# Recurrence of an RWKV-7 / attention hybrid block: products without state gathered, VectorE order pinned, preparing bursts placed behind scan steps

## Chip, core and metric

The kernel runs on one core of one Trainium2 chip. The metric is the device time of one launch in microseconds. Before the change three runs took 1697.61, 1698.09 and 1704.32 us; the median is 1698.09.

The engines of the core work from queues of their own: TensorE (PE; its weight loads are shown as PEld), VectorE (DVE), ScalarE (ACT), GpSimd (POOL) and SyncE (SP), which here only issues transfers. Each works its queue in order and waits on semaphores.

## What is computed

One transformer block over 1024 tokens of width 1024, batch 1: a modulated RMS norm, a large input projection, eight heads of causal attention with a forget gate, eight heads of an RWKV-7 recurrence, gated merging, and a convolutional feed-forward net. All inputs are float32. The change touches the recurrence alone:

```python
def step(state, inp):
    r_t, w_t, k_t, v_t, a_t, b_t = inp
    sa = jnp.einsum('bhvk,bhk->bhv', state, a_t)
    state = state * w_t[:, :, None, :] + sa[..., None] * b_t[:, :, None, :] + v_t[..., None] * k_t[:, :, None, :]
    y_t = jnp.einsum('bhvk,bhk->bhv', state, r_t)
    return state, y_t
...
_, y = lax.scan(step, state0, (tm(r_h), tm(w_h), tm(k_h), tm(v_h), tm(a_vec), tm(b_vec)))
```

The state of a head is a 64 x 64 matrix.

## The kernel before

**Units and chunks.** The recurrence is computed by chunks of 64 tokens. A unit is a pair of heads (`p`, 0 to 3) and half of the sequence (`hf`), so there are eight units, numbered `k`, each of eight chunks (`NCU`). The two heads of a pair lie on partitions 0 to 63 and 64 to 127 (`HS`). Within a chunk all depends on matrices that can be made without the state; the state then passes from chunk to chunk in a short serial scan.

**Two chains.** A unit has two parts, written as Python generators that emit instructions and yield a wait in nanoseconds of a planned clock:

- `pre(k, p, hf)` prepares. It loads the decays (`cum`, L738) and makes their running sum by a scan instruction on DVE (L741); normalises the keys (product `ssq`, then a row of full-size DVE operations, L757 to L773); makes the in-chunk products (`p`, two bursts, L782 to L791); sends the diagonal blocks through DRAM (`sm` to `M32`, L796 to L801), inverts the triangular 32 x 32 blocks in 31 steps of two DVE operations (`t`, L809, and `E`, L811), and sends the inverses back through DRAM (`se` to `TT`, L822); transposes (`vt`, `at`, `tb`), and makes `q` and `bs`. Its waits are 1275, 3400, 10500, 2200, 2200, 2000 and 3400 ns.
- `main(k, p, hf)` uses them. It transposes the inverse's blocks on DVE (`X`, L866), waits for the time `ready` that `pre` had set (its own time plus 46000 for the first unit, 38500 for the others, L802), finishes the inverse (`xi`, `zi`), makes `uw` and `mz`, whose results DVE adds into `Zt` and `Mt` (L904, L905), and runs the scan over chunks. Then come the group norm's sums `mu` and `va`. Its waits are 2360, 2000, 2970, 2400, seven of 1150, 700, 3400, 2700 and 3400 ns.

**A step of the scan.** The next state is `(sp)*pcd`, where `sp` accumulates in PSUM a product without state, `E` by `UV`, and one with it, `Mt` by `S0`; DVE scales it (S, L929). The output `yp` is accumulated likewise from `UV` by `E` and `S0` by `Zt`. The function `fixed(c)` issues the four products without state of chunk c (two heads, `sp` and `yp`): chunk 0's behind `mz`, chunk c + 1's behind the wait of 1150 that follows step c. `sp` and `yp` are one PSUM bank each.

**Who decides the order.** PE's order is the order of emission, made by the planner `Weave`: `now` is a planned clock that `mm` and `transpose` advance by fixed costs (L67 to L75, L142). `run` serves the chain that is due, the main chain first; when none is due, `fill` emits products of large projections from a queue (`rkv`, `qk`, `v` and gate projections, 213 ns of the planned clock for one of 512 columns) until the next is due. In that clock a group of `fixed` costs 320, the state products of a step 213, `xi` and `zi` 427 each, `uw` and `mz` 1707 each. A preparing chain may run at most two units ahead (`passed`), and waits with filling until its three projections are there (`got`). The orders on DVE, ACT and POOL are not written out here: the framework chooses them, under the data's dependencies and those that are added by hand (`add_manual_dep` without a semaphore, which fixes an order on one engine).

**After the recurrence** come attention, which takes the gate projections that are left between its own steps, and then the merge and the feed-forward net.

Of the kernel before, what the change touches and what calls it, by code (L numbers as in the profile page):

```python
# [12 lines left out]
ALU = mybir.AluOpType  # L13
# [10 lines left out]
NCU = NH // CH  # L24
# [11 lines left out]
NOSYNC = mybir.DependencyInfo(mybir.DependencyClass.NoSync, mybir.DependencyReason.DATA)  # L36
# [11 lines left out]
class Weave:  # L48
# [27 lines left out]
    def add(self, load, run):  # L76
        self.queue.append((load, run))

    def prefetch(self):
        while (self.first or self.queue) and len(self.loaded) < 1:  # L80
            load, run = (self.first or self.queue).popleft()
            self.loaded.append((load(), run))
# [30 lines left out]

        self.live.append([self.now + wait, 0, chain])

    def run(self, chains):

        self.live = [[self.now, 1 + i, g] for i, g in enumerate(chains)]
        while self.live:
            due = min((c for c in self.live if c[0] <= self.now), key=lambda c: (c[1], c[0]), default=None)  # L120
            if due is None:
                self.fill(min(c[0] for c in self.live))
                continue
            wait = next(due[2], None)
            if wait is None:
                self.live.remove(due)
            else:
                due[0] = self.now + max(wait, 0.0)
# [3 lines left out]
def hybrid_block(ctx: ExitStack, tc: tile.TileContext, a, out):  # L132
    nc = tc.nc
    weave = Weave()
    ctx.enter_context(tc.manual_schedule(engines={mybir.EngineType.PE}))

    def mm(o, lhsT, rhs, start, stop, more=False):

        weave.mm_cost(o, lhsT, rhs)
        nc.tensor.matmul(o, lhsT, rhs, start=start, stop=stop, skip_group_check=more)  # L140
# [8 lines left out]
    tt, stt, ts = nc.vector.tensor_tensor, nc.vector.scalar_tensor_tensor, nc.vector.tensor_scalar  # L149
# [19 lines left out]
    def C(name):  # L169
        o, k = CST[name]  # L170
        return cst[:, o : o + k] if o < NC1 else cst2[:, o - NC1 : o - NC1 + k]
# [163 lines left out]
    with ExitStack() as es:  # L335
# [26 lines left out]
        def rkv_items(p, hf):  # L362
            ts_ = {x: rkp.tile([128, NH], F32, tag=f"{x}{hf}", name=f"{x}{p}{hf}") for x in "rkv"}
            rkv[p, hf], got[p, hf] = [ts_[x] for x in "rkv"], 0

            def steps(w, x, t):
                if hf == 0:
                    last_col[p, x] = shp.tile([128, 1], F32, tag=f"pv{x}", name=f"pv{p}{x}")
                yield from shifted(w, t, hf, ts_[x], last_col[p, x], f"rkv{t}")
                got[p, hf] += 1  # L370

            for x, t in (("k", 4 + p), ("r", p), ("v", 8 + p)):
                yield (lambda t=t: w_in(12 + t)), (lambda w, x=x, t=t: steps(w, x, t))
# [16 lines left out]
        HS = (slice(0, 64), slice(64, 128))  # L390
# [318 lines left out]
            return ap.rearrange("p (c x) -> p c x", x=x)  # L709

        BKS = (slice(0, 2), slice(1, 3))
        state, units, passed = {}, {}, set()

        blk_r = rw.tile([128, 128], F32R, name="blk_r")
        nc.scalar.copy(blk_r, C("blk"))
# [9 lines left out]
        def pre(k, p, hf):  # L725
# [5 lines left out]
            def tmp(nm, w=NH, bufs=1, dt=F32):  # L731
                return rw.tile([128, w], dt, tag=nm, name=f"{nm}{n}", bufs=bufs)

            def chunk_tile(nm, bufs, *dims):
                return rw.tile([128, *dims], F32, tag=nm, name=f"{nm}{n}", bufs=bufs)

            cum = tmp("cum")
            nc.sync.dma_start(cum, d_lora[0, p, :, cs])  # L738
            al = tmp("al")
            nc.sync.dma_start(al, d_lora[1, p, :, cs])  # L740
            nc.vector.tensor_tensor_scan(cum, C("reset"), cum, initial=0.0, op0=ALU.mult, op1=ALU.add)  # L741
            el = chunk_tile("el", 1, NCU, CH + 1)
            nc.gpsimd.memset(el[:, :, 0:1], 1.0)
            nc.scalar.activation(el[:, :, 1:], c3(cum), AF.Exp, scale=-DEC)
# [25 lines left out]
            pcd = chunk_tile("pcd", 3, NCU)  # L770
# [8 lines left out]
            E = chunk_tile("E", 2, NCU, 2, 3, CH)  # L779
            QA = chunk_tile("QA", 2, NCU, 2, CH)  # L780
            UV = chunk_tile("UV", 2, NCU, 2, CH)
            for c0 in range(0, NCU, 4):  # L782
                ps = [gen(f"p1_{n}{h}{c0}") for h in range(2)]
                for c in range(c0, c0 + 4):
                    for h in range(2):
                        mm(ps[h][:, (c - c0) * 128 : (c - c0) * 128 + 128], bk[HS[h], c, BKS[h], :], ar[HS[h], :, c, :],
                           start=True, stop=True)
# [11 lines left out]
            M32 = chunk_tile("M32", 1, 32, 32)  # L799
            for g in range(4):  # L800
                nc.sync.dma_start(M32[g * 32 : g * 32 + 32, :, :], sm.rearrange("h c b s t -> (h c b) s t"))  # L801
            ready = weave.now + (46000 if k == 0 else 38500)  # L802
            E32 = chunk_tile("E32", 1, 8, 32)
            nc.gpsimd.tensor_copy(E32, C("einit").rearrange("p (j t) -> p j t", t=32))
            t32 = tmp("t32", 256)
            for s in range(31):
                J, W = s // 4 + 1, 31 - s
                tv = t32[:, 0 : J * W].rearrange("p (j w) -> p j w", w=W)
                tt(tv, E32[:, 0:J, s : s + 1].to_broadcast([128, J, W]),  # L809
                   M32[:, s : s + 1, s + 1 : 32].to_broadcast([128, J, W]), op=ALU.mult)  # L810
                tt(E32[:, 0:J, s + 1 : 32], E32[:, 0:J, s + 1 : 32], tv, op=ALU.add)  # L811
            se = scr.tile([2, NCU, 2, 32, 32], F32, tag="se", name=f"se{n}")
            for g in range(4):
                nc.sync.dma_start(
# [2 lines left out]
            TT = chunk_tile("TT", 2, NCU, CH)  # L817
# [37 lines left out]
        def main(k, p, hf):  # L855
# [3 lines left out]
            pcd, ar, E, QA, TT, bon, UV = (o[k] for k in ("pcd", "ar", "E", "QA", "TT", "bon", "UV"))  # L859


            X = rw.tile([128, NCU, 32], F32, tag="X", name=f"X{n}", bufs=1)
            B0 = (slice(0, 32), slice(64, 96))
            B1 = (slice(32, 64), slice(96, 128))
            for h in range(2):
                nc.vector.transpose(X[B0[h], :, :], TT[B0[h], :, 0:32])  # L866
            yield max(0, o["ready"] - weave.now)
            xi = gen(f"xi{n}")
            for c in range(NCU):
# [25 lines left out]
            Zt = rw.tile([128, NCU, CH], F32, tag="Zt", name=f"Zt{n}", bufs=1)  # L895
            Mt = rw.tile([128, NCU, CH], F32, tag="Mt", name=f"Mt{n}", bufs=1)
# [11 lines left out]
            yp = py.tile([128, NCU, CH], F32, tag="yp", name=f"yp{n}")  # L908
            sp = py.tile([128, NCU, CH], F32, tag="sp", name=f"sp{n}")
            S0 = state.get(p)  # L910

            def fixed(c):

                alone = hf == 0 and c == 0
                for h in range(2):
                    mm(sp[HS[h], c, :], E[:, c, h, 2, :], UV[:, c, h, :], start=True, stop=alone)
                for h in range(2):
                    mm(yp[HS[h], c, :], UV[:, c, h, :], E[:, c, h, 1, :], start=True, stop=alone)

            fixed(0)  # L920
            yield 2400
            for c in range(NCU):
                if S0 is not None:
                    for h in range(2):
                        mm(sp[HS[h], c, :], Mt[HS[h], c, :], S0[HS[h], :], start=False, stop=True)
                S1 = None
                if not (hf == 1 and c == NCU - 1):
                    S1 = rw.tile([128, CH], F32, tag="state", name=f"S{n}{c}", bufs=3)
                    ts(S1, sp[:, c, :], pcd[:, c : c + 1], None, op0=ALU.mult)  # L929
                if S0 is not None:  # L930
                    for h in range(2):
                        mm(yp[HS[h], c, :], S0[HS[h], :], Zt[HS[h], c, :], start=False, stop=True)
                if c + 1 < NCU:
                    yield 1150
                    fixed(c + 1)
                S0 = state[p] = S1
            passed.add((k, 1))

# [53 lines left out]
        def pre_chain():  # L992
            for k, (p, hf) in enumerate(order):
                while got[p, hf] < 3:
                    weave.step()
                yield from pre(k, p, hf)
                if p < 3:
                    weave.first.extend(rkv_items(p + 1, hf))
                yield 0

        def main_chain():
            for k, (p, hf) in enumerate(order):
                while (p, hf) not in units:
                    yield 200
                yield from main(k, p, hf)
                yield 0

        weave.run([main_chain(), pre_chain()])
    rk_st.close()


# [307 lines left out]
    for x in range(2):  # L1319
        for n in range(8):  # L1320
            if x or n:
                k = 8 * x + n + 1
# [157 lines left out]
    due = []  # L1480
# [248 lines left out]
    units = [(k, j) for k in ORDER for j in range(NP)]  # L1729
# [265 lines left out]
```

## Time and profile before

| quantity | value |
|---|---|
| median of three runs | 1698.09 us (1697.61 to 1704.32) |
| the profiled execution: time, span | 1704.73 us, 1703.0 us |
| mean granted TensorE clock | 0.983 |
| instructions | 26042 |
| recurrence, 160 to 657 us: PE busy | 479.29 of 497 us |
| attention, 657 to 869 us: PE busy | 199.46 of 212 us |
| merge and feed-forward, 869 to 1703 us: PE busy | 826.24 of 834 us |

How rows are read. A row of the timeline has the start in us, the duration, engine, source line, operation, out<-in by the program's names, shapes, and the number of instructions merged; in square brackets is the idle time of the engine just before, and what ended it. A row of a table of waits has who waited for whom, the total in us, the number of waits and the longest. A row of a table of windows has the window, its length, busy time with instruction count of PE, PEld, DVE, ACT and POOL, then the granted clock of PE, the DMA engines' share, and GB/s. A float32 product appears as two matmul instructions. A matmul's duration holds its latency; products in a row overlap, so their pace is the distance of their starts. L140 is the one line that issues all products but the transposes, so products are told apart by their names.

### The profile page before, as it was taken

The page shows a single profiled execution, that of the slowest core. Times are in us where ns is not written, and L with a number is a line of the kernel's source. Part 1 is how long each engine was busy: PE and PEld are TensorE (multiplying, and loading weights), DVE is VectorE, ACT ScalarE, POOL GpSimd, SP SyncE. Part 2 cuts the span into 40 slices and gives each one's busy share as a digit, 9 for nine tenths or more (in the row PEclk, how much of TensorE's full clock was granted, in tenths as well). Part 3 has the DMA queues.
Part 4 walks back from the last instruction along what each step waited for, and adds up shares of the span by engine and source line. Part 5 has one row for each costly group of instructions (what it writes and reads, how often), then busy time and mean ns, then how long its engine had stood idle before and what let it go on. Part 6 is the DMA issues. An engine that isn't in the chain of part 4 may idle for free.

```text
span 1703.0 us, 26042 instructions
## 1 busy us (share of the span) xinstructions
PE 1638.0 (96%) x9772; PEld 1342.0 (79%) x9772; DVE 1220.8 (72%) x2390; ACT 808.6 (47%) x1482; POOL 143.4 (8%) x175
## 2 busy tenths in 40 slices
PE   5899999998999998999999999999999999999998
PEld 4767777786877776988878888888888888888886
DVE  5776787778676633888877634897777777787677
ACT  5453334333444554766642323654444444454455
POOL 0010101110111003123112000000000000000000
PEclk8899999999999999999999999999999999999999
DMA  8487743533342326433277611132333233484463
GB/s 328 139 314 205 192 125 97 136 106 106 91 115 75 91 81 151 141 110 107 76 265 268 246 62 63 50 105 94 123 107 103 93 117 101 163 284 153 125 215 112
DMA packets 120974, 239.85 MB, mean 141 GB/s; under 512 B 39888, under 2 KB 48336, under 8 KB 120848
## 3 DMA queue, kind: packets, MB, share of 16 engines
q1 hardware_dynamic: 112896, 220.94, 40.0%
q0 software_dynamic: 7952, 17.25, 3.8%
q8 instruction: 77, 1.26, 0.3%
q14 instruction: 49, 0.40, 0.1%
HBM read 172.59 MB, written 65.54 MB: 140 GB/s over the span
## 4 chain that ended last, share of the span: by engine, by line
PE 79%; DVE 9%; DMA 6%; ACT 2%; issue 2%; SPq 1%; DVEq 0%; ACTq 0%
PE X L140 13%; PE D L140 12%; PE Y L140 6%; PE wo L140 5%; PE br L140 5%; PE gt L140 5%; PE rk_ps L140 4%; PE qk L140 4%; PE ps_rkv L140 4%; PE W L140 3%; PE lg L140 2%; PE v L140 2%; PE ov L140 2%; PE sp L140 2%; PE tp L144 2%
## 5 line engine op out<-in xcount | busy, mean ns | idle before, releaser
L140 PE MATMUL D<-op,op 128*128 128x512 f32 x924 | 209.8, 390 | 0.0
L140 PEld LDWEIGHTS D<-op,op 128*128 128x128 f32 x924 | 173.5, 188 | 36.2 <-DVE op L1258 0.3
L140 PE MATMUL X<-T_m,S 128*128 128x512 f32 x440 | 107.3, 390 | 0.2
L140 PEld LDWEIGHTS X<-T_m,S 128*128 128x128 f32 x440 | 82.5, 188 | 18.2 <-ACT x L1534 0.6
L1257 ACT CAST op<-g 128x512 fp32r<-128x512 f32 x77 | 47.8, 621 | 74.1 <-PE D L140 48.0
L1258 DVE TENSOR_TENSOR op<-g,op 128x512 fp32r<-128x512 f32 x77 | 53.0, 689 | 41.7 <-ACT op L1257 41.7
L1494 DVE SCALAR_TENSOR_TENSOR c<-ab,vec,c 128x512 f32<-128x512 f32 x88 | 65.9, 750 | 19.5 <-ACT c L1497 17.9
L809 DVE TENSOR_TENSOR t<-E,M 128x60 f32<-128x60 f32 (+24 forms) x248 | 57.9, 233 | 30.2 <-DMA M<-sm 24.9
L1458 DVE TENSOR_TENSOR S<-ur,S 128x512 fp32r<-128x512 f32 x66 | 45.5, 691 | 35.6 <-ACT S L1454 35.5
L263 DVE TENSOR_TENSOR lo_in<-raw_in,hi_in 128x512 fp32r<-128x512 f32 x84 | 56.5, 707 | 16.1 <-PE gt L140 13.9
L1454 ACT CAST S<-ur 128x512 fp32r<-128x512 f32 x66 | 41.0, 622 | 55.6 <-DVE ur L1447 30.6
L1458 DVE TENSOR_TENSOR A<-ur,A 128x512 fp32r<-128x512 f32 x64 | 44.1, 688 | 30.9 <-ACT A L1454 30.7
L261 ACT CAST hi_in<-raw_in 128x1024 fp32r<-128x1024 f32 x42 | 44.0, 1049 | 44.3 <-PE ps_rkv L140 16.0
L140 PE MATMUL Y<-T_h,A 128*128 128x512 f32 x264 | 63.5, 390 | 0.0
L140 PE MATMUL Y<-T_h,S 128*128 128x512 f32 x264 | 63.3, 390 | 0.0
L140 PE MATMUL X<-B_b,A 128*128 128x512 f32 x252 | 60.8, 391 | 0.0
L140 PE MATMUL W<-B_f,A 128*128 128x512 f32 x252 | 60.6, 390 | 0.0
L1079 ACT ACTIVATE P<-lg,nm 128x896 f32<-128x896 f32 (+3 forms) x64 | 47.4, 743 | 22.8 <-DVE nm L1075 22.6
L811 DVE TENSOR_TENSOR E<-E,t 128x60 f32<-128x60 f32 (+24 forms) x248 | 53.8, 217 | 5.8
L140 PEld LDWEIGHTS Y<-T_h,A 128*128 128x128 f32 x264 | 49.6, 188 | 10.3
L140 PEld LDWEIGHTS Y<-T_h,S 128*128 128x128 f32 x264 | 49.6, 188 | 10.3
L1454 ACT CAST A<-ur 128x512 fp32r<-128x512 f32 x64 | 39.9, 623 | 34.2 <-PE X L140 31.5
(473 smaller groups left out, 4169.0 us busy)
## 6 DMA issues: line engine op xcount, KB each, us to landing
raw_in<-in_w_in SPq DMA_DIRECT2D x50, 512.0 KB, 3.7
wm<-in_w_mod SPq DMA_DIRECT2D x48, 512.0 KB, 7.0
ur<-in_w_up SPq DMA_DIRECT2D x44, 512.0 KB, 4.2
g<-d_g SPq DMA_DIRECT2D x35, 512.0 KB, 4.0
d_g<-gs SPq DMA_DIRECT2D x44, 256.0 KB, 2.0
d_g<-c SPq DMA_DIRECT2D x33, 256.0 KB, 4.4
d_st<-qh SPq DMA_DIRECT2D x64, 128.0 KB, 2.5
d_gate<-gs SPq DMA_DIRECT2D x32, 256.0 KB, 2.9
```

Of the source, the lines that this page charges most:

```text
L140: nc.tensor.matmul(o, lhsT, rhs, start=start, stop=stop, skip_group_check=more)
L144: nc.tensor.transpose(o, i, eye)
L261: nc.scalar.copy(hi, raw)
L263: nc.vector.tensor_tensor(lo[:, c : c + NH], raw[:, c : c + NH], f32(hi[:, c : c + NH]), op=ALU.subtract)
L809: tt(tv, E32[:, 0:J, s : s + 1].to_broadcast([128, J, W]), M32[:, s : s + 1, s + 1 : 32].to_broadcast([128, J, W]), op=ALU.mult)
L811: tt(E32[:, 0:J, s + 1 : 32], E32[:, 0:J, s + 1 : 32], tv, op=ALU.add)
L1079: nc.scalar.activation(e[:, 0:n], lg[:, 0:n], AF.Exp, bias=nm[:, 0:1], accum_out=nm[:, 1:2])
L1257: nc.scalar.copy(hi, src)
L1258: tt(lo, src, f32(hi), op=ALU.subtract)
L1454: nc.scalar.copy(hi, src)
L1458: tt(lo, src, f32(hi), op=ALU.subtract)
L1494: stt(c, ab[:, x + hf * NH : x + hf * NH + NH], V("conv_w", 22 * x + i), c, op0=ALU.mult, op1=ALU.add)
```

## The change

Six edits, all in the recurrence and the planner:

- The products without state of all eight chunks are issued in one go behind `mz`, ahead of the wait of 2400; between two steps only the wait of 1150 is left. As they now all come before the first product that accumulates on them, only chunk 0's opens its bank (`start=c == 0`).
- The two transposes `X` of unit k (from the second unit on) must follow, on DVE, the last state S of the unit before.
- The decay scan of unit k (from the second on) must follow, on DVE, step 11 of the inverse of the unit before.
- The first unit's `ready` is 48500 instead of 46000.
- `Weave.run` has an argument `beside`, 2600 for the recurrence: if the main chain is due within that time and no main step has been emitted since the last filling, a due preparing chain is held, the time up to the main step is filled, and the preparing burst comes right behind that step.
- `skip_group_check` on the scan's products concerns a check at build time and changes no instruction.

```diff
-    def run(self, chains):
+    def run(self, chains, beside=0.0):
         self.live = [[self.now, 1 + i, g] for i, g in enumerate(chains)]
+        led = False
         while self.live:
             due = min((c for c in self.live if c[0] <= self.now), key=lambda c: (c[1], c[0]), default=None)
-            if due is None:
-                self.fill(min(c[0] for c in self.live))
+            lead = min((c[0] for c in self.live if c[1] < 2), default=None)
+            if due is None or (due[1] > 1 and not led and lead is not None and lead < self.now + beside):
+                self.fill(min(c[0] for c in self.live) if due is None else lead)
+                led = False
                 continue
+            led = beside > 0 and (led or due[1] < 2)
             wait = next(due[2], None)
...
-            nc.vector.tensor_tensor_scan(cum, C("reset"), cum, initial=0.0, op0=ALU.mult, op1=ALU.add)
+            i = nc.vector.tensor_tensor_scan(cum, C("reset"), cum, initial=0.0, op0=ALU.mult, op1=ALU.add)
+            if k:
+                tc.add_manual_dep(i.ins, placed["inverse"].ins.name, NOSYNC)
...
-            ready = weave.now + (46000 if k == 0 else 38500)
+            ready = weave.now + (48500 if k == 0 else 38500)
...
-                tt(E32[:, 0:J, s + 1 : 32], E32[:, 0:J, s + 1 : 32], tv, op=ALU.add)
+                i = tt(E32[:, 0:J, s + 1 : 32], E32[:, 0:J, s + 1 : 32], tv, op=ALU.add)
+                if s == 11:
+                    placed["inverse"] = i
...
             for h in range(2):
-                nc.vector.transpose(X[B0[h], :, :], TT[B0[h], :, 0:32])
+                i = nc.vector.transpose(X[B0[h], :, :], TT[B0[h], :, 0:32])
+                if k:
+                    tc.add_manual_dep(i.ins, placed["state"].ins.name, NOSYNC)
...
-            def fixed(c):
+            for c in range(NCU):
                 alone = hf == 0 and c == 0
                 for h in range(2):
-                    mm(sp[HS[h], c, :], E[:, c, h, 2, :], UV[:, c, h, :], start=True, stop=alone)
+                    mm(sp[HS[h], c, :], E[:, c, h, 2, :], UV[:, c, h, :], start=c == 0, stop=alone, more=True)
                 for h in range(2):
-                    mm(yp[HS[h], c, :], UV[:, c, h, :], E[:, c, h, 1, :], start=True, stop=alone)
-            fixed(0)
+                    mm(yp[HS[h], c, :], UV[:, c, h, :], E[:, c, h, 1, :], start=c == 0, stop=alone, more=True)
             yield 2400
             for c in range(NCU):
...
-                    ts(S1, sp[:, c, :], pcd[:, c : c + 1], None, op0=ALU.mult)
+                    placed["state"] = ts(S1, sp[:, c, :], pcd[:, c : c + 1], None, op0=ALU.mult)
...
                 if c + 1 < NCU:
                     yield 1150
-                    fixed(c + 1)
...
-        weave.run([main_chain(), pre_chain()])
+        weave.run([main_chain(), pre_chain()], beside=2600.0)
```

More of the change, by code (lines that the diff above doesn't have):

```diff
@@ L711, in hybrid_block @@
         BKS = (slice(0, 2), slice(1, 3))
-        state, units, passed = {}, {}, set()
+        state, units, passed, placed = {}, {}, set(), {}
         blk_r = rw.tile([128, 128], F32R, name="blk_r")
@@ L924, in main @@
                     for h in range(2):
-                        mm(sp[HS[h], c, :], Mt[HS[h], c, :], S0[HS[h], :], start=False, stop=True)
+                        mm(sp[HS[h], c, :], Mt[HS[h], c, :], S0[HS[h], :], start=False, stop=True, more=True)
                 S1 = None
@@ L928, in main @@
                     S1 = rw.tile([128, CH], F32, tag="state", name=f"S{n}{c}", bufs=3)
-                    ts(S1, sp[:, c, :], pcd[:, c : c + 1], None, op0=ALU.mult)
+                    placed["state"] = ts(S1, sp[:, c, :], pcd[:, c : c + 1], None, op0=ALU.mult)
                 if S0 is not None:
                     for h in range(2):
-                        mm(yp[HS[h], c, :], S0[HS[h], :], Zt[HS[h], c, :], start=False, stop=True)
+                        mm(yp[HS[h], c, :], S0[HS[h], :], Zt[HS[h], c, :], start=False, stop=True, more=True)
                 if c + 1 < NCU:
                     yield 1150
-                    fixed(c + 1)
                 S0 = state[p] = S1
```

## Prediction

> **What bounds the kernel now.** I read the page first, then the recurrence (160 to 657 us) by windows, by TensorE's waits, and by the timelines of TensorE (PE) and VectorE (DVE) around the longest waits.
>
> ```profile
> span 1703.0 us, 26042 instructions
> PE 1638.0 (96%) x9772; PEld 1342.0 (79%) x9772; DVE 1220.8 (72%) x2390; ACT 808.6 (47%) x1482; POOL 143.4 (8%) x175
> ```
>
> PE sets the pace. In the recurrence it is kept full by projection products (`ps_rkv`, `qk`, `v`, `gt`) that the planner pours into every planned wait, and that work must be done anyway. So a shorter or longer plan only moves projections from one stage to another; time is won where PE really stands still, or where the same products take PE longer. The waits of PE from 157 to 657 us, with total, count and longest:
>
> ```profile
> PE sp L140 <- DVE S L929: 8.6, 5, 3.5
> PE xi L140 <- DVE X L866: 3.0, 2, 1.6
> PE p L140 <- DVE bk L769: 2.0, 1, 2.0
> PE ps_rkv L140 <- DVE k L358: 1.6, 1, 1.6
> PE at L144 <- DVE E L789: 1.0, 1, 1.0
> ```
>
> Every one of them is for DVE, whose queue is in a fixed order. Its own idle time in the same stretch says why it is late:
>
> ```profile
> DVE t L809 <- DMA M<-sm: 24.9, 7, 6.7
> DVE X L866 <- DMA TT<-se: 23.3, 12, 4.9
> DVE cum L741 <- DMA cum<-d_lora: 10.8, 5, 5.5
> ```
>
> The worst place, DVE and then PE:
>
> ```profile
> 421.72 0.43 DVE L866 STREAM_TRANSPOSE X<-TT 32x256 f32<-32x256 f32 x1 [3.80 <-DMA TT<-se]
> 423.68 0.28 DVE L929 TENSOR_SCALAR S<-sp,pcd 128x64 f32<-128x64 f32 x1
> 424.02 0.47 PE L140 MATMUL sp<-UV,E 128*64 128x64 f32 x4 [3.46 <-DVE S L929]
> ```
>
> The next unit's transpose X stands in DVE's queue ahead of this unit's state S and waits 3.80 us for a transfer; S is behind it, and PE stands for 3.46 us. The second such place costs 2.35 us:
>
> ```profile
> 532.86 0.34 PE L140 MATMUL sp<-UV,E 128*64 128x64 f32 x4 [2.35 <-DVE S L929]
> ```
>
> And an idle PE pays again:
>
> ```profile
> 420.00:424.00 4.00, 0.56 (x3) 0.13 (x1) 2.22 (x6) 1.22 (x2) 0.00 (x0) 1.00 0.17 25
> 424.00:428.00 4.00, 3.98 (x26) 2.96 (x28) 2.33 (x5) 0.71 (x2) 0.00 (x0) 0.57 0.17 60
> 529.00:533.00 4.00, 1.65 (x10) 1.04 (x12) 1.43 (x4) 1.24 (x2) 0.40 (x1) 1.00 0.42 98
> 533.00:537.00 4.00, 4.00 (x30) 2.78 (x28) 3.57 (x7) 1.25 (x2) 0.00 (x0) 0.57 0.17 66
> 230.00:232.50 2.50, 0.28 (x6) 0.20 (x7) 2.13 (x5) 0.00 (x0) 0.00 (x0) 1.00 0.60 139
> 232.50:237.00 4.50, 4.50 (x40) 3.63 (x41) 3.75 (x14) 1.96 (x5) 0.19 (x1) 0.62 0.48 152
> ```
>
> These windows come in pairs: a stretch with a hole in PE at clock 1.00, then one at 0.57 or 0.62. The lost clock is 4 x 0.43 = 1.7 us, 1.7 us and 4.5 x 0.38 = 1.7 us.
>
> On the clock, the Trainium skill ("TensorE: Matmul & The Clock Gate", section "HAM oscillation — how this bites in real kernels") says not to leave gaps of more than about 3.4 us. By it only the 3.46 us hole would have cost clock, and the sum below would be 3.4 us smaller, ending near 1687. The trace differs: the clock fell after 2.35 us too (window 533 to 537 at 0.57), so I go by the windows.
>
> **The change part by part.** Sums are made against the profiled execution, 1704.73 us (span 1703.0).
>
> *Transposes X behind the last state.* No instruction is added; the two transposes of the next unit must follow the last L929 of this one. Both big holes go: 3.46 + 2.35 = 5.8 us and 2 x 1.7 = 3.4 us of clock. What is late next is X itself. In unit 3:
>
> ```profile
> 320.63 1.16 PE L140 MATMUL p<-ar,bk 64*128 64x128 f32 x16
> 371.39 0.44 DVE L866 STREAM_TRANSPOSE X<-TT 32x256 f32<-32x256 f32 x1 [0.55 <-DMA TT<-se]
> 380.59 0.69 PE L140 MATMUL xi<-X,E 32*32 32x32 f32 x32
> ```
>
> X is ready 8.8 us ahead of its user, 51.2 us after the second `p` burst that begins its chain of transfers and DVE steps. That is the cover. **-9.2 us.**
>
> *First unit's due time 46000 to 48500.* PE waits 3.0 us at `xi` (table of waits) and loses 1.7 us of clock (232.5 to 237). A product of 512 columns is 213 ns in the planner, so 2500 more are 12 products; on the chip 8 of them take 1.81 us:
>
> ```profile
> 656.95 1.98 PE L140 MATMUL rk_ps<-u_hi,hi_in 128*128 128x512 f32 x8
> 658.76 1.98 PE L140 MATMUL rk_ps<-u_lo,hi_in 128*128 128x512 f32 x8
> ```
>
> So 12 x 0.226 = 2.7 us of wanted work takes the place of 2.7 of the 3.0 us. **-4.4 us** with the clock.
>
> *Decay scan behind the inverse's step 11.* The `ps_rkv` wait of 1.6 us comes from here:
>
> ```profile
> 393.11 1.23 DVE L741 TENSOR_TENSOR_SCAN cum<-cst,cum 128x512 f32<-128x512 f32 x1 [2.98 <-DMA cum<-d_lora]
> 395.70 0.74 DVE L358 SCALAR_TENSOR_TENSOR k<-ps_rkv,omu,sh_rkv 128x512 f32<-128x512 f32 x1
> 396.36 0.22 DVE L811 TENSOR_TENSOR E<-E,t 128x69 f32<-128x69 f32 x1
> ```
>
> DVE stood 2.98 us for the scan's input, and the eviction of k behind it was late. The inverse was then at step 8 (69 = 3 x 23 elements), so step 11 lies past the landing and the scan no longer waits. Its two readers, the exponentials on ScalarE (ACT), are wanted only some microseconds later. **-1.6 us** (0 if the wait moves).
>
> *All products without state in one go.* Nothing is added: each unit still issues eight groups of four `sp`/`yp` products, now behind `mz`. One step and a burst, before:
>
> ```profile
> 316.06 0.34 PE L140 MATMUL sp<-UV,E 128*64 128x64 f32 x4
> 316.23 0.29 PE L140 MATMUL yp<-E,UV 128*64 128x64 f32 x4
> 316.44 0.33 PE L140 MATMUL sp<-S,Mt 64*64 64x64 f32 x4
> 316.61 0.28 PE L140 MATMUL yp<-Zt,S 64*64 64x64 f32 x4
> 316.82 1.16 PE L140 MATMUL p<-ar,bk 64*128 64x128 f32 x16
> 328.26 1.15 PE L140 MATMUL q<-UV,E 64*64 64x64 f32 x32
> 329.34 0.50 PE L140 MATMUL va<-Zts,blk_r 128*128 128x512 f32 x1
> ```
>
> A fixed group takes 316.44 - 316.06 = 0.38 us (eight matmul instructions, two to a float32 product), eight of them 3.04. In one stream the bounds are 3.04 (nothing saved) and the rate of `q`, 1.08 us for 32, so 2.16 for 64. I take the rate of the `sp` half, 0.17 for 4, so 2.7, being the same products: 0.35 per unit, **-3 us** over eight units (0 to -7). The fixed group no longer waits for the S before it; the state product does, behind the same planned 1150. The planner's sum is unchanged: 8 x 320 + 2400 ahead and 7 x 1150 within, against 320 + 2400 and 7 x (1150 + 320). So Zt and Mt get 2.2 us more cover, and a step shrinks by 0.38 us, from about 2.35 to 1.97.
>
> *Preparing bursts beside steps.* A burst of the lower chain now waits for the next step of the main chain if that is due within 2600. With its own costs and waits the preparing chain of a unit is 31.0 in the planner's units (waits 25.0, products 6.0), the main chain 37.4. Eight pieces held by about 1.3 each make 41: it then takes longer than the main chain and slips by 3 to 4 a unit from unit 3 on, eating the 8.8 us of cover, until the due time of 38500 holds the main chain back and projections fill. What remains can be an X late by 0 to 2.5 us in some of units 4 to 7: **+2 us** (0 to +17). Where a burst lies directly behind other short products, one way in and out of the projections is saved, about 0.1 us a side (the first two projections behind a step took 0.57 us, rows below, not 2 x 0.226). That can be so for `tb`/`q` behind `xi`: **-1 us** (0 to -2).
>
> ```profile
> 265.19 0.73 PE L140 MATMUL ps_rkv<-u_hi,hi_in 128*128 128x512 f32 x2
> 265.76 1.09 PE L140 MATMUL ps_rkv<-u_lo,hi_in 128*128 128x512 f32 x4
> ```
>
> *What stays.* The stage's planned length hardly changes, so I take the same number of gate projections in it; one more or fewer (48 products of 0.226, 10.9 us) moves between stages without changing PE's sum. The other three state waits, 8.6 - 5.8 = 2.8 us, come from full-size DVE steps of the next unit between two states; I leave them as they are (0 to -2.8, or worse: rival B). The 2.0 at `p` and 1.0 at `at` stay.
>
> Sum: -5.8 - 3.4 - 4.4 - 1.6 - 3 + 2 - 1 = **-17 us**, 1687.5 on the profiled execution. That execution is 6.6 us above the median of the runs, 1698.09, and just above the slowest, 1704.32. If the 6.6 is made of the very waits for transfers that go, the runs win 17 - 6.6 = 10.6; if it lies elsewhere, 17. So 1681 to 1687.5; I take **1684**.
>
> **Rivals.**
>
> *A, the late preparing chain.* X misses its user in units 4 to 7 by about 2.5 us each, and each hole costs 1.7 us of clock: 4 x 4.2 = 17, so 1701. For it: 51.2 us from `p` to X against a due time of 38.5 in the planner's units; a whole unit of 37.4 lasts 50.6 us on the chip (from the row below to `xi` at 380.59), so 38.5 is about 52: hardly any margin. Against: a DVE that no longer stands for X runs the inverse faster.
>
> ```profile
> 330.00 0.69 PE L140 MATMUL xi<-X,E 32*32 32x32 f32 x32
> ```
>
> *B, the slower side: DVE sets the scan.* DVE in two scan windows:
>
> ```profile
> 302.70:316.80 14.10, 14.10 (x135) 10.04 (x132) 11.51 (x40) 3.44 (x5) 1.28 (x1) 1.00 0.48 119
> 467.20:481.70 14.50, 14.50 (x172) 12.05 (x171) 13.51 (x46) 4.35 (x7) 1.28 (x1) 1.00 0.36 109
> ```
>
> In the second DVE is busy 13.51 of 14.5 us, and the steps are to be a sixth shorter. If DVE holds the steps at 2.35 us, PE idles 0.38 in 56 steps, 21 us: 1705. It decides for slower from 0.40 us a step (22.6 us above 1684); with one more 0.7 us operation ahead of each S it is 39 us, 1723. Against: the burst gives DVE 2.2 us ahead of the scan, and in the first window DVE is busy 11.51 of 14.1 us.
>
> *C, the waits only move.* The transfers are no earlier; DVE waits for TT or M elsewhere, and other evictions are late. The X and scan terms (10.8) halve and the stream saves nothing: 1684 + 5.4 + 3 = 1692.
>
> **How the numbers follow.** Forecast 0.60, A 0.12, B 0.12, C 0.16. For this kernel 0.5% is 8.5 us: faster is below 1689.6, slower above 1706.6. The forecast's own range is 1676 to 1691, so 0.56 of its 0.60 is faster; C gives 0.04 more, and the rest of C, of the forecast and A make 0.27 within; B, nearly all slower, with a little of A makes 0.13. The low end, 1672, has the stream at -7, the state waits gone and no new `xi` wait (-4 - 2.8 - 2 from 1681, rounded); the high end, 1702, takes in A and C.
>
> **What would show it.** After the change no X should wait in DVE's queue ahead of an S, and no window of the recurrence should have a clock under 1.00. The stream behind `mz` should take about 2.7 us and a step about 1.97. `xi` waits in units 4 to 7 would show A; many short `sp` waits for S, B. If the two holes go and the time stands, the error is in what I count as PE's own pace.

## The result, and the profile after

| | before | after |
|---|---|---|
| median, same chips | 1700.68 us (1697.61 to 1704.32, 4 runs) | 1719.43 us (1718.50 to 1721.73, 4 runs) |
| profiled execution, span | 1703.0 us | 1716.7 us |

The ratio is 1.011, with a 95% interval of 1.0088 to 1.0131: slower by 18.8 us in the medians, 35 us above the forecast and 17 above the top of its range.

The same stages by windows, before and then after. The first window is the recurrence, up to the end of its last gate projection (a gate, for short); the second is attention, up to the first product of the merge. The columns are window, length, busy time and count of PE, PEld, DVE, ACT and POOL, clock, DMA share and GB/s.

```profile
160.00:657.10 497.10, 479.39 (x4319) 382.18 (x4318) 336.43 (x963) 212.25 (x371) 57.82 (x79) 0.99 0.40 112
657.10:868.90 211.80, 199.28 (x1201) 173.84 (x1199) 164.27 (x323) 140.34 (x318) 49.64 (x61) 0.97 0.41 114
868.90:1703.00 834.10, 826.32 (x3700) 684.01 (x3700) 610.23 (x942) 374.62 (x669) 22.72 (x16) 1.00 0.42 144
```

```profile
160.00:672.50 512.50, 491.44 (x4403) 395.23 (x4402) 345.22 (x967) 222.45 (x387) 57.91 (x79) 0.98 0.39 111
672.50:881.00 208.50, 184.78 (x1104) 161.70 (x1103) 159.42 (x320) 130.43 (x298) 41.51 (x51) 0.94 0.37 106
881.00:1716.70 835.70, 828.00 (x3700) 684.72 (x3700) 610.33 (x942) 374.54 (x669) 23.26 (x16) 0.99 0.42 143
```

The recurrence is 15.4 us longer, attention 3.3 us shorter, the rest 1.6 us longer: 13.7 us, the difference of the spans. That is 5 us less than the medians differ, because the profiled execution of before, 1704.73 us, was slower than its other runs and the one of after, 1718.50, the fastest of its four. And the stages no longer hold the same work: by the counts attention has lost 97 matmul instructions and the recurrence gained 84; most of the difference had run ahead of 160 us already:

```profile
0.00:160.00 160.00, 133.00 (x556) 101.94 (x557) 109.86 (x165) 81.39 (x126) 13.21 (x20) 0.91 0.73 252
```

```profile
0.00:160.00 160.00, 135.92 (x568) 104.52 (x569) 110.68 (x167) 82.72 (x128) 13.66 (x20) 0.93 0.74 256
```

The gates emitted in the recurrence, before and after (the row has busy time, mean in ns, and the idle time before):

```profile
L140 PE MATMUL gt<-u_hi,hi_in 128*128 128x512 f32 x144 | 40.7, 407 | 0.0
```

```profile
L144 PE MATMUL gt<-u_hi,hi_in 128*128 128x512 f32 x176 | 47.8, 400 | 0.4 <-DVE r L362 0.4
```

A gate has 16 products of this kind (and 32 of the other two), so it is nine gates before and eleven after, with seven and five left for attention. Two gates are 96 x 0.226 = 21.7 us of PE. The recurrence took 84 x 0.226 = 19.0 us more work in 15.4 us, so it has saved only 3.6 us of its own. Attention gave up 21.7 us of work and got 3.3 us shorter: PE's idle time in it rose from 12.5 to 23.7 us, and its busy time fell by 14.5 us instead of 21.7, at a lower clock (0.97, then 0.94). Some of its waits, before and then after (who for whom, total us, count, longest):

```profile
PE rk_ps L140 <- ACT gm L1180: 4.7, 2, 4.5
PE ov L140 <- DVE o L1148: 3.2, 2, 2.2
PE lg L140 <- ACT P L1079: 0.6, 2, 0.4
```

```profile
PE ov L144 <- DVE o L1154: 7.3, 4, 2.3
PE rk_ps L144 <- ACT gm L1186: 4.6, 2, 4.4
PE lg L144 <- ACT P L1085: 3.6, 3, 1.9
PE ov L144 <- DVE tl L1121: 2.6, 3, 2.0
```

PE waits there for results of the softmax on ACT and DVE; gates fill PE between attention's own products. The last gate product of attention began at 859.5 us before and at 818.6 after. Two windows of 25 us from that part of the stage, before and then after:

```profile
800.00:825.00 25.00, 25.00 (x162) 22.43 (x161) 21.05 (x44) 19.33 (x44) 8.99 (x12) 1.00 0.43 128
825.00:850.00 25.00, 23.61 (x145) 20.42 (x144) 18.89 (x42) 15.14 (x38) 0.90 (x1) 1.00 0.06 22
```

```profile
816.00:841.00 25.00, 18.83 (x121) 17.22 (x120) 20.57 (x43) 16.35 (x37) 6.01 (x7) 0.92 0.33 97
841.00:866.00 25.00, 18.86 (x100) 16.46 (x99) 15.77 (x36) 11.28 (x30) 0.00 (x0) 0.84 0.00 1
```

With gates PE is busy 48.6 of 50 us; without them 37.7, and the clock falls to 0.92 and 0.84.

Why two more gates? The projections that a preparing chain needs are put at the head of the queue when an earlier preparing chain ends, behind what is running and what is already loaded. Whenever a queued projection starts, the next one is taken from the queue and loaded. Unit 3's preparation ends with `bs`. Before, then after, on PE's timeline:

```profile
334.43 0.50 PE L140 MATMUL bs<-cum,blk_r 128*128 128x512 f32 x1
334.77 0.40 PE L140 MATMUL bs<-en,blk_r 128*128 128x512 f32 x1
...
340.02 0.28 PE L140 MATMUL v<-hi_v,u_hi 128*128 128x256 f32 x1
```

```profile
332.97 1.11 PE L144 MATMUL v<-hi_v,u_hi 128*128 128x256 f32 x8
...
339.89 0.50 PE L144 MATMUL bs<-cum,blk_r 128*128 128x512 f32 x1
340.23 0.39 PE L144 MATMUL bs<-en,blk_r 128*128 128x512 f32 x1
```

Before, `bs` came ahead of the start of the first `v` projection, so what was loaded at that start was unit 5's. After, `bs` came 7 us behind it: the second `v` was loaded already and went ahead of the projections of unit 5. These ran from 416 us, not 382. All later units were late, three gates and not one slipped in ahead of the last set of unit projections, and the recurrence could not end before that set was used. Rows from the first and the last of these sets, before and then after:

```profile
382.51 1.78 PE L140 MATMUL ps_rkv<-u_hi,hi_in 128*128 128x512 f32 x7
...
515.79 1.98 PE L140 MATMUL ps_rkv<-u_hi,lo_in 128*128 128x512 f32 x8
```

```profile
416.22 2.00 PE L144 MATMUL ps_rkv<-u_hi,hi_in 128*128 128x512 f32 x8
...
514.22 2.00 PE L144 MATMUL ps_rkv<-u_hi,hi_in 128*128 128x512 f32 x8
```

The last products of the last set began at 515.79 before; after, its first began at 514.22.

The edits on DVE's order did much of what was expected. From 157 to 680 us after the change, DVE's idle time for M and TT, and PE's three largest waits:

```profile
DVE t L815 <- DMA M<-sm: 26.5, 7, 6.0
DVE X L874 <- DMA TT<-se: 13.2, 7, 4.1
```

```profile
PE sp L144 <- DVE S L936: 7.1, 5, 3.0
PE mz L144 <- ACT UV L903: 4.3, 1, 4.3
PE p L144 <- DVE bk L775: 2.7, 2, 1.5
```

X's idle time fell from 23.3 to 13.2 us, the decay scan's from 10.8 to 0.2, and the wait at `xi` is gone. But waits for S are still 7.1 us, and a new one stands at `mz`. There the late preparing chain makes it: the inverse, with its wait for M, now falls between `uw` and `mz`. On DVE:

```profile
388.64 0.19 DVE L815 TENSOR_TENSOR t<-E,M 128x31 f32<-128x31 f32 x1 [5.30 <-DMA M<-sm]
388.87 0.19 DVE L817 TENSOR_TENSOR E<-E,t 128x31 f32<-128x31 f32 x1
389.10 0.19 DVE L815 TENSOR_TENSOR t<-E,M 128x30 f32<-128x30 f32 x1
389.20 0.42 DVE L901 COPY Wt<-uw 128x256 f32<-128x256 f32 x1
```

The second Wt, which `mz` needs, stands behind the inverse's first operations, and these wait 5.30 us for M. The copy UV on ACT, which the table names, came later still: in the trace it waits 5.54 us for that Wt.

### The profile page after: what moved, and what is told of

It is laid out like the page before. It is cut to its first block, busy times and chain, and to the rows that moved or that the text cites. A ratio compares the mean times of both kernels' runs of the same rounds, so it can differ in the third digit from the quotient of the medians.

```text
span 1716.7 us, 26060 instructions
## 1 busy us (share of the span) xinstructions
PE 1640.1 (96%) x9772; PEld 1346.2 (78%) x9772; DVE 1225.6 (71%) x2394; ACT 810.1 (47%) x1480; POOL 136.3 (8%) x165
## 4 chain that ended last, share of the span: by engine, by line
PE 60%; DVE 6%; ACT 2%; DMA 1%; issue 1%; SPq 0%; DVEq 0%; ACTq 0%
PE X L144 13%; PE D L144 12%; PE Y L144 6%; PE wo L144 5%; PE br L144 5%; PE gt L144 5%; PE W L144 3%; PE rk_ps L144 3%; PE lg L144 2%; PE ov L144 2%; PE tp L148 2%; DVE nm L1081 1%; DVE P L1091 1%; PE tr L144 1%; DVE tl L1121 1%
## 5 line engine op out<-in xcount | busy, mean ns | idle before, releaser
L1263 ACT CAST op<-g 128x512 fp32r<-128x512 f32 x77 | 47.8, 621 | 74.0 <-PE D L144 47.5
L267 DVE TENSOR_TENSOR lo_in<-raw_in,hi_in 128x512 fp32r<-128x512 f32 x88 | 60.6, 723 | 27.8 <-PE gt L144 12.2
L1081 DVE TENSOR_REDUCE nm<-lg 128x1 f32<-128x896 f32 (+3 forms) x64 | 46.8, 752 | 14.5 <-PE lg L144 13.7
```

The costliest lines, as they stand in the source:

```text
L267: nc.vector.tensor_tensor(lo[:, c : c + NH], raw[:, c : c + NH], f32(hi[:, c : c + NH]), op=ALU.subtract)
L1081: nc.vector.tensor_reduce(nm[:, 0:1], lg[:, 0:n], axis=AX.X, op=ALU.max, negate=True)
L1263: nc.scalar.copy(hi, src)
```

## The experiments

Two theories stood against each other. G: the loss is attention's, which has lost two gates to a changed order of projections. H: the loss is in the recurrence, in waits that the holding of preparing bursts makes. "Held" below means that the bursts wait for a main step, as in the change. The number of gates in the recurrence is known ahead for each kernel from its order of emission.

**Two gates early, in the kernel before.**

```diff
-    while len(weave.queue) > 12:
+    while len(weave.queue) > 4:
```

> The kernel before, with one number changed: two more gate projections (96 products) are emitted between the recurrence and attention, so attention is left with five of them, as in the kernel after, instead of seven. Nothing in the recurrence differs. Theory G (the loss of the change is attention's lost filler): the two gates cost 96 x 0.226 = 21.7 us ahead of attention and attention gets only about 3 us shorter, so 1700.7 + 18 = 1719 (1714 to 1723). Theory H (the loss sits in the recurrence, in waits that the held preparing bursts make): work that only moves costs nothing, 1700.7 within 4.

Measured 1724.15 us against 1699.01 (ratio 1.0153, 1.013 to 1.0176): +25 us. That is 7 us more than G's 18 and just above its range, and far from H's nothing: gates moved ahead of attention are not free. Attention's window, from the end of the last gate ahead of it:

```profile
683.30:886.10 202.80, 182.79 (x1105) 160.06 (x1104) 157.88 (x317) 130.34 (x298) 40.08 (x50) 0.95 0.30 91
```

Attention shrank by 9 us here (211.8 to 202.8) for the 21.7 us of work taken from it. The stretch ahead of it grew by 26.2 us (523.3 against 497.1), with a wait of PE of 3.9 us for an eviction on DVE among the moved gates. So the two profiled executions (1721.89 and 1704.73 us) differ by 17 us, close to G's 18, and the medians by 25; the profiled one of before is slower than most of its runs.

**The kernel after with 46000.**

```diff
-            ready = weave.now + (48500 if k == 0 else 38500)
+            ready = weave.now + (46000 if k == 0 else 38500)
```

> The kernel after with the first unit's due time put back to 46000; the bursts are still held. By the order of emission nine gates then lie in the recurrence again, not eleven. Theory G: 1719.4 - 18 for the gates + 4.4 for the first unit's xi wait that comes back = 1706 (1700 to 1710). Theory H: the holding is still there and the xi wait comes back, so 1719 to 1726.

Measured 1690.96 us (ratio 0.9954, 0.994 to 0.9969). The kernel is faster than before, with the holding in it. H as the whole cause falls: its range began 28 us higher. G's number was 15 us too high as well. It took 18 us for the gates where the run above shows 25, and the `xi` wait that came back was 1.3 us, not 3.0; that is not all of the 15.

**The kernel after without holding.**

```diff
-        weave.run([main_chain(), pre_chain()], beside=2600.0)
+        weave.run([main_chain(), pre_chain()])
```

> The kernel after without the holding of preparing bursts (beside 0); gathered products, both orders on VectorE and 48500 stay. Nine gates in the recurrence by the order of emission. Theory G: 1719.4 - 18 = 1701, less what the gathered products and the orders save without holes made by the holding, so 1690 to 1701. Theory H: the same direction; only a time above 1710 would speak against both.

Measured 1680.45 us (ratio 0.9889, 0.9873 to 0.9905), 10 us below G's low end. Timed once more:

> The kernel after without holding, timed again on the chip of the run beside it: 1680 within 3.

Measured 1679.37 us against 1700.73 (ratio 0.9886, 0.9862 to 0.9909). This beats both kernels. Its recurrence and attention, and its three largest waits from 157 to 655 us:

```profile
160.00:632.20 472.20, 464.23 (x4306) 372.58 (x4306) 336.65 (x960) 211.05 (x369) 58.55 (x79) 1.00 0.41 116
632.20:840.70 208.50, 196.59 (x1200) 171.66 (x1199) 164.42 (x323) 140.38 (x318) 49.16 (x61) 0.98 0.40 115
```

```profile
PE rk_ps L144 <- ACT gm L1186: 3.6, 2, 3.0
PE p L144 <- DVE bk L775: 2.7, 2, 1.5
PE sp L144 <- DVE S L936: 2.2, 3, 1.0
```

The stage is 24.9 us shorter than before with the same nine gates (some 3 us of it had run ahead of 160 us, 13 instructions by the counts), its clock is 1.00, and the waits for S are 2.2 us. Attention takes 208.5 us, the same length as after the change, with 96 products more in it.

Set beside the kernel after, this shows that G is not all. The recurrence after is 40.3 us longer (512.5 against 472.2). Two gates are 21.7 of these; the other 18.6 us were lost inside the recurrence, where PE idles 21.1 us instead of 8.0 and the clock is 0.98.

**Holding alone, in the kernel before** (only the planner's loop and `beside=2600.0`).

> The kernel before with nothing but the holding of preparing bursts (beside 2600). Nine gates in the recurrence by the order of emission. Theory G: no great change, 1700.7 within 6, since the number of gates is that of before. Theory H: the holding itself makes waits, 1708 to 1720.

Measured 1701.27 us (ratio 1.0011, 1.0002 to 1.0021): +2 us, as G has it. In the kernel before holding costs little where the order of projections stays.

**Either side of the change of order.** The kernel after with two due times 500 ns apart.

```diff
-            ready = weave.now + (48500 if k == 0 else 38500)
+            ready = weave.now + (47000 if k == 0 else 38500)
```

> The kernel after with the first unit's due time 47000 in place of 48500; all else as in after. By the order of emission the second set of projections for unit 5 then comes ahead of the second v projection again, and nine gates lie in the recurrence. Theory G (attention's lost filler): like the run with 46000, with a smaller xi wait, 1686 to 1692. Theory H (the loss comes smoothly from holding together with a late first unit): between 1691 (46000) and 1719 (48500) by the distance, 1000 of 2500 ns, so about 1702.

Measured 1689.93 us (ratio 0.9939, 0.9915 to 0.9964), inside G's range.

> The same with 47500, 500 ns more in the planner than its neighbour. By the order of emission eleven gates lie in the recurrence. Theory G: a jump of about 25 us (the price measured for two gates emitted early), 1711 to 1720. Theory H: 500 ns are worth at most 6 us, about 1708 or less.

Measured 1712.07 us (ratio 1.0068, 1.0048 to 1.0088), inside G's range again. Half a microsecond in the planner cost 22 us. In the profiled executions the recurrence grew from 482.5 to 500.6 us and attention shrank only from 209.4 to 205.5. The end of unit 3's preparation and the `v` projections, with 47000 and then with 47500:

```profile
336.93 0.50 PE L144 MATMUL bs<-cum,blk_r 128*128 128x512 f32 x1
337.26 0.39 PE L144 MATMUL bs<-en,blk_r 128*128 128x512 f32 x1
...
337.72 1.11 PE L144 MATMUL v<-hi_v,u_hi 128*128 128x256 f32 x8
```

```profile
329.47 0.40 PE L144 MATMUL v<-hi_v,u_hi 128*128 128x256 f32 x2
...
333.71 0.50 PE L144 MATMUL bs<-cum,blk_r 128*128 128x512 f32 x1
334.04 0.39 PE L144 MATMUL bs<-en,blk_r 128*128 128x512 f32 x1
```

With 47000 `bs` came just ahead of the first `v` product; with 47500 `v` had begun 4.2 us earlier. This is the step between nine gates and eleven, and a smooth cost of holding would not make it. The last 1000 ns, from 47500 to 48500, add 7 us more (1712.1 to 1719.4) at eleven gates in both.

**Gathering alone, in the kernel before** (`fixed` for all chunks behind `mz`, as in the change).

> The kernel before with only the products without state gathered behind mz. Nine gates. In the trace of after the eight groups took 1.9 us in a stream, against 0.38 each before: 3.05 - 1.9 = 1.15 us less a unit, so theory S (stream) expects -9 us, 1690 (1686 to 1694). Theory B (VectorE sets the scan, as in the prediction): the shorter steps come back as waits for S, 1699 or more.

Measured 1691.38 us against 1699.51 (ratio 0.9954, 0.9936 to 0.9973): -8 us, as S has it. DVE did not take over the scan: PE's waits for S were 7.4 us, against 8.6 before.

**The two orders alone, in the kernel before** (both `add_manual_dep`).

> The kernel before with only the two orders on VectorE (transposes X behind the last state, decay scan behind step 11). Nine gates. The prediction's terms: -9.2 for the two holes and their clock, -1.6 for the scan: 1688 (1685 to 1691). Theory C (the waits only move): half of it or less, 1694 to 1699.

Measured 1688.34 us (ratio 0.9937, 0.9916 to 0.9959): -11 us, the size that was expected. PE's waits for S and X in the recurrence:

```profile
PE sp L140 <- DVE S L935: 4.8, 5, 2.2
PE xi L140 <- DVE X L870: 1.3, 1, 1.3
```

The waits for S fell by 3.8 us (from 8.6), not by 5.8; the wait at `xi`, which stood in another term, fell by 1.7. So the total fits better than its parts, and that is partly luck.

**48500 alone, in the kernel before.**

> The kernel before with only the first unit's due time at 48500. Nine gates. The prediction's term was -4.4 (the xi wait of 3.0 us with 1.7 us of clock, less 0.3 that stays): 1695 (1693 to 1697). If the clock loss is not real or another wait takes its place: 1698 or more.

Measured 1701.30 us against 1700.73 (ratio 1.0003, 0.999 to 1.0016): nothing. The `xi` wait is gone and another, of 4.0 us, is there:

```profile
231.26 2.93 PE L140 MATMUL qk<-u_hi,hi_in 128*128 128x512 f32 x6 [4.04 <-DVE v L358]
```

PE now reaches a PSUM buffer that the eviction of v had not freed: that eviction stands on DVE just behind the late X, at 230.45 us, and ends as PE goes on. The extra filling only met DVE's lateness elsewhere.

**Gathering and orders without the other two** (the kernel after, `beside=0`, 46000).

> The kernel after without holding (beside 0) and with 46000: the gathered products and the two orders alone. Nine gates. If the parts add: 1699.5 - 8.1 - 11.2 = 1680, and with 48500 on top (the earlier run, 1680.5) nothing more was won. If 48500 was worth its 4.4 there: 1684 to 1686 here. With this run the four of holding and due time are complete.

Measured 1684.91 us (ratio 0.991, 0.9884 to 0.9936). With 48500 beside it on the same chip 1679.37: here the due time was worth 5.5 us. The four combinations of holding and due time, with gathering and orders in all:

| | 46000 | 48500 |
|---|---|---|
| not held | 1684.9 | 1679.4 |
| held | 1691.0 | 1719.4 |

Held, the due time costs 28 us; not held, it saves 5.5. The four were not all timed together; the kernels before beside them lay within 2 us of each other.

## Why the prediction was wrong

- **The step that failed** is in the part "What stays": the planned length hardly changes, so the same number of gate projections lies in the recurrence, and "one more or fewer ... moves between stages without changing PE's sum". The number was eleven, not nine. PE's sum did stay (busy 1638.0 us before, 1640.1 after), but the time is not PE's sum: attention cannot use the time that the gates leave, so it becomes idle time, and two gates cost 25 us in the kernel before. The profile of before had the hint: attention's PE is busy 199 of 212 us with 76 us of gates in it (7 x 48 x 0.226), so without them it must idle.
- **Preparing bursts beside steps**, +1 us in the sum, was mis-sized and mis-placed. That the preparing chain slips was right, and so was the reason: with 48500 unit 3's `bs` came at 339.89 us held and at 329.59 not held. But I priced the slip by X against its cover (rival A, 17 us), not by what else hangs on the chain's end, which is the place of the next projections in the queue, nor by the inverse that now falls into the main chain. The waits at `xi` that would have shown A did not come. In the runs holding costs 2 us alone, 6 with gathering and orders (1691.0 against 1684.9), and 40 with 48500 as well; in the profiles that is about 22 for the two gates and 19 inside the recurrence.
- **Transposes and decay scan** (-9.2 and -1.6, together -10.8): measured -11.2. The mechanism and the total were right, the split between the waits was not (above).
- **Gathering** (-3, bounds 0 to -7): measured -8.1. The mechanism was right; the stream takes about 2.0 us for 64 matmul instructions (after: first at 289.99, next projection at 292.00), 31 ns each, faster than the 34 of `q` which I took as the lower bound. A step did come out as forecast: 1.96 us from one state product to the next (after: 299.51 to 301.48), for 1.97.

```profile
289.99 0.34 PE L144 MATMUL sp<-UV,E 128*64 128x64 f32 x4
...
292.00 1.42 PE L144 MATMUL qk<-u_lo,hi_in 128*128 128x512 f32 x5
```

- **48500** (-4.4): 0 alone, -5.5 with gathering and orders beside it, and +28 where bursts are held, most of it at the step in the order of projections.
- **Rival B** (DVE sets the scan) fell with gathering alone. **Rival C** (waits only move) fell for the orders, but describes 48500 alone well.
- Where the order of projections stayed, the held kernels won 8 us (46000) and 10 us (47000), about half of the sum's 17, and the kernel without holding 21. So the size of the sum was not confirmed for the kernel that it was made for.

What is not shown: that in the kernel after, with 48500 and 2600 unchanged, restoring the order of projections alone would give two gates' worth of time back. No run did that; the pair 500 ns apart and the two gates moved in the kernel before stand for it. Which waits make up the 18.6 us inside the recurrence, beyond those at S and `mz`, is open too.

## What to carry to other kernels

Filler work is not neutral: before calling a moved piece free, ask whether the stage it leaves can still keep the engine busy. Where a queue takes new work "behind what is running or loaded", a small delay of the one who adds it can change the order of everything behind; compare the emission orders of the two kernels before trusting a sum of durations. And try such edits in pairs: holding and the later due time were nearly free each, and together cost all that the others had won, and 19 us more.

## What the runs showed of the hardware

The gathered small products ran faster than in the trace of before: 31 ns for each 128 x 64 by 64 matmul instruction in one stream, against 47.5 in groups of eight between products of other tile shapes (0.38 us). In the recurrence of the fastest kernel, where PE's waits for one source add up to 2.7 us at most, the granted clock was 1.00 over 472 us, against 0.99 before.
